# Output projection of a hybrid decoder layer by Strassen's form over quarters

## The chip, the cores and the metric

The kernel runs on one core of a Trainium2 chip. The metric is the device time of one execution in microseconds. A core has five engines with queues of their own, each of which takes its instructions strictly in order: TensorE (PE, matmuls, with PEld for the weight loads), VectorE (DVE), ScalarE (ACT), GpSimd (POOL) and SyncE (SP, which here only issues transfers). They wait for each other by semaphores. SBUF holds the operands; matmul results come in PSUM, in eight banks of 128 x 512 floats.

## The reference

One layer over 1024 tokens of width 1024, in float32. What matters here is the last product of the mixer: the outputs of eight softmax heads (NSA, 512 features) and of four gated linear-attention heads (GLA, 512 features) are joined and multiplied by one 1024 x 1024 matrix.

```python
x = x + 0.5 * swiglu_ffn(rmsnorm(x, g1), w_gate1, w_up1, w_down1)
x = x + hybrid_mixer(rmsnorm(x, gm), w_in, ..., w_out)
#     hybrid_mixer ends with
#     return jnp.concatenate([o_nsa, o_gla], axis=-1) @ w_out
x = x + 0.5 * swiglu_ffn(rmsnorm(x, g2), w_gate2, w_up2, w_down2)
return rmsnorm(x, final_norm)
```

## The kernel before

Every tensor of activations lies with features on partitions and tokens along the free axis, in two halves of 512 tokens. Each float32 operand is held as two tiles, a high part (`hi`, written by ACT as a rounded copy) and a low part (`lo`, the remainder, written by DVE as source minus high). `mm3` (L209) makes of each product three matmuls of 128 x 128 by 128 x 512: high by high, high by low, low by high.

The program runs five stages in order: FFN1 (by Strassen's form over quarters already, its weights as sums in several stages), the input projection, attention with GLA beside it, the output projection, FFN2 (Strassen's form again) with the final norm. There is no automatic scheduler: the order on every engine is the order in which the Python code issues instructions. Side work is written as generators, kept in `self.side`; `tick` steps them between blocks of matmuls, so that a `yield` puts the next step one tick later in all queues. `later(n)` puts the next n weight tiles into the queue, `fetch` starts a weight tile's load into one of three raw buffers and has ACT write the highs (L238), `settle` has DVE write the lows (L247). A weight tile is used from a ring; a slot of it is free when PE has read it for the last time.

The output projection is the loop L2246 to L2281. For each token half, and each of eight tiles of 128 output features, `fm` makes 8 x 3 matmuls into one PSUM bank, 384 in all (24 of them run early, in the attention's last part, for the GLA features, and are kept in `part`). DVE then adds the bank to the residual x (L2254), POOL adds the early part to two tiles (L2256), ACT squares the result and DVE adds the squares up (`squares`, L266 and L270) for the norm of FFN2. The tokens of half 1 are joined on the way (`joined`: high and low summed, L1482, and split anew, L1485 and L1488).

When half 0 is finished, its norm (`norm`, `rms`, `normed`) runs as side work under the matmuls of half 1. PE sums the squares over partitions (L286), DVE scales the sum (L291), POOL takes the power (L293), PE spreads it over partitions (L298), and DVE multiplies x by gain and factor (L322), then ACT and DVE split the result (L330, L331). `second` runs this for half 0 and then for half 1. FFN2's weights begin with the products for the A12 quarter, whose input is half 0 alone, so that the norm of half 1 runs under them. In FFN2, ACT L453 and DVE L456 split the weights.

## Time and profile before

| what | value |
|---|---|
| median of 3 runs | 1911.36 us (1911.22 to 1911.61) |
| the profiled execution's own time | 1911.64 us |
| its span | 1909.8 us |
| ACT busy | 46% |
| POOL busy | 11% |
| mean DMA traffic | 170 GB/s |
| attention's matmuls end | 1181.6 us |
| projection's first matmul after them to FFN2's first matmul | 1181.6 to 1264.1 us |

The span is the time from the first instruction's start to the last one's end, on the slowest core; the execution lasts 1.8 us longer than it. In a row of the profile, out<-in names the written and read tiles, "128*128" is the matmul's weight form, xN is the number of instructions, and what stands in brackets is the idle time ahead of it and what ended it. In the projection the transfers are the weights (512 KB a tile), the residual x, the joined head outputs and the stores of x.

### The profile page before, as it was taken

The page shows a single profiled execution, that of the slowest core. Times are in us where ns is not written, and L with a number is a line of the kernel's source. Part 1 is how long each engine was busy: PE and PEld are TensorE (multiplying, and loading weights), DVE is VectorE, ACT ScalarE, POOL GpSimd, SP SyncE. Part 2 cuts the span into 40 slices and gives each one's busy share as a digit, 9 for nine tenths or more (in the row PEclk, how much of TensorE's full clock was granted, in tenths as well). Part 3 has the DMA queues.
Part 4 walks back from the last instruction along what each step waited for, and adds up shares of the span by engine and source line. Part 5 has one row for each costly group of instructions (what it writes and reads, how often), then busy time and mean ns, then how long its engine had stood idle before and what let it go on. Part 6 is the DMA issues. An engine that isn't in the chain of part 4 may idle for free. (4 is left out here: it accounts for less than half of the span.)

```text
span 1909.8 us, 26312 instructions
## 1 busy us (share of the span) xinstructions
PE 1895.9 (99%) x9291; PEld 1562.8 (82%) x9291; DVE 1375.4 (72%) x2302; ACT 883.7 (46%) x1697; POOL 202.6 (11%) x259
## 2 busy tenths in 40 slices
PE   9999999999999999999999999999999999999998
PEld 7888888888888888778887888888888888888887
DVE  7977778886876762554878887557777777767766
ACT  6633333344544551323478877335333333344443
POOL 0000000000000010121445553000000000000001
PEclk9999999999999999999999999999999999999999
DMA  7434456668865230119473324544333455688652
GB/s 261 150 129 140 149 193 215 215 229 305 314 232 176 89 103 27 56 45 254 135 231 95 103 71 132 205 160 160 130 126 125 146 197 198 221 294 300 230 177 89
DMA packets 173860, 325.00 MB, mean 170 GB/s; under 512 B 17920, under 2 KB 49792, under 8 KB 173216
## 3 DMA queue, kind: packets, MB, share of 16 engines
q1 hardware_dynamic: 165152, 308.35, 47.2%
q0 software_dynamic: 2720, 10.23, 1.7%
q10 hardware_dynamic: 5856, 4.75, 0.8%
q8 instruction: 73, 1.20, 0.3%
q14 instruction: 59, 0.48, 0.1%
HBM read 234.62 MB, written 92.86 MB: 171 GB/s over the span
## 5 line engine op out<-in xcount | busy, mean ns | idle before, releaser
L211 PE MATMUL bank<-T,wt 128*128 128x512 f32 x704 | 273.9, 389 | 0.0
L212 PE MATMUL bank<-T,wt 128*128 128x512 f32 x704 | 273.9, 389 | 0.0
L213 PE MATMUL bank<-T,wt 128*128 128x512 f32 x704 | 273.9, 389 | 0.0
L211 PE MATMUL bank<-bd,wd 128*128 128x512 f32 (+1 forms) x632 | 243.0, 385 | 0.0
L213 PE MATMUL bank<-bd,wd 128*128 128x512 f32 (+1 forms) x632 | 242.5, 384 | 0.0
L212 PE MATMUL bank<-bd,wd 128*128 128x512 f32 (+1 forms) x632 | 242.5, 384 | 0.0
L211 PE MATMUL bank<-h,wt 128*128 128x512 f32 x536 | 210.1, 392 | 1.0 <-ACT wt L453 1.0
L213 PE MATMUL bank<-h,wt 128*128 128x512 f32 x536 | 209.0, 390 | 0.2
L212 PE MATMUL bank<-h,wt 128*128 128x512 f32 x536 | 208.6, 389 | 0.0
L634 ACT ACTIVATE g<-bank 128x512 f32<-128x512 f32 x88 | 52.6, 598 | 266.1 <-PE bank L213 266.0
L211 PEld LDWEIGHTS bank<-T,wt 128*128 128x128 f32 x704 | 132.2, 188 | 27.6
L213 PEld LDWEIGHTS bank<-T,wt 128*128 128x128 f32 x704 | 132.1, 188 | 27.4
L212 PEld LDWEIGHTS bank<-T,wt 128*128 128x128 f32 x704 | 132.2, 188 | 27.2
L213 PEld LDWEIGHTS bank<-bd,wd 128*128 128x128 f32 x632 | 118.8, 188 | 23.6
L212 PEld LDWEIGHTS bank<-bd,wd 128*128 128x128 f32 x632 | 118.8, 188 | 23.5
L211 PEld LDWEIGHTS bank<-bd,wd 128*128 128x128 f32 x632 | 118.8, 188 | 22.9
L453 ACT ACTIVATE wt<-v 128x512 fp32r<-128x512 f32 x176 | 109.7, 623 | 46.4 <-DVE v L418 30.1
L211 PE MATMUL bank<-h,w 128*128 128x512 f32 x312 | 124.2, 398 | 0.0
L456 DVE TENSOR_TENSOR wt<-v,wt 128x512 fp32r<-128x512 f32 x176 | 120.5, 685 | 3.5 <-ACT wt L453 3.5
L213 PE MATMUL bank<-h,w 128*128 128x512 f32 x312 | 121.8, 390 | 0.0
L212 PE MATMUL bank<-h,w 128*128 128x512 f32 x312 | 121.5, 389 | 0.0
L211 PEld LDWEIGHTS bank<-h,wt 128*128 128x128 f32 x536 | 100.7, 188 | 22.9 <-ACT wt L453 2.4
(284 smaller groups left out, 3759.7 us busy)
## 6 DMA issues: line engine op xcount, KB each, us to landing
in<-in_w_f_dram SPq DMA_DIRECT2D x132, 256.0 KB, 5.3
in<-b SPq DMA_DIRECT2D x132, 256.0 KB, 5.4
raw<-in_w_f_dram SPq DMA_DIRECT2D x44, 512.0 KB, 4.7
up<-in_w_f_dram SPq DMA_DIRECT2D x44, 512.0 KB, 5.4
raw<-in_w_in_dram SPq DMA_DIRECT2D x23, 512.0 KB, 3.8
raw<-in_w_f_dram SPq DMA_DIRECT2D x44, 256.0 KB, 4.1
b<-g SPq DMA_DIRECT2D x44, 256.0 KB, 2.1
l<-tb SPq DMA_DIRECT2D x22, 512.0 KB, 5.7
```

The source lines that it names most:

```text
L211: mm(ps, w[0], x[0], start=first, stop=False, skip_group_check=True)
L212: mm(ps, w[0], x[1], start=False, stop=False, skip_group_check=True)
L213: mm(ps, w[1], x[0], start=False, stop=last, skip_group_check=True)
L453: nc.scalar.activation(t[:, 0], a, AF.Copy)
L456: nc.vector.tensor_tensor(t[:, 1], a, t[:, 0].bitcast(F32), OP.subtract)
L634: nc.scalar.activation(dst, src, AF.Copy)
```

## The change

The projection becomes Strassen's form (in Winograd's arrangement) over the four quarters of tokens and features. With two halves of tokens and two of features (NSA and GLA), the inputs are the quarters "11" (NSA of half 0), "22" (GLA of half 1), "12" (NSA of half 1), and the sums T1 (GLA of half 0 less GLA of half 1), T3 (NSA of half 0 less GLA of half 0), T2 (T3 plus GLA of half 1) and T4 ("12" less T2). Seven products of 4 tiles x 4 contraction blocks x 3 matmuls, 48 each, take the place of eight. The code runs them in the order 1, 3, 6, 5, 7, 2, 4; product 1 has only two tiles in this stage, since the other two run early as before. A "block" here is one output tile of one product, 12 matmuls; there are 26 (1 and 2 of "22", 3 to 6 of "11", 7 to 10 of T2, 11 to 14 of T1, 15 to 18 of T3, 19 to 22 of "12", 23 to 26 of T4). Each product enters one or two quarters of x, so there are 36 additions from PSUM instead of 16, and 8 additions of `part` on POOL instead of 2.

The weight sums are taken by POOL in FFN1's second stage (`sum_up`), written to DRAM, and loaded from there: 13 weight tiles instead of 10, in a ring of four. The token sums T1, T3 and T2 are taken by POOL in the attention (`differences`) and written to DRAM; the projection's `prepare` loads them and splits them into high and low. T4, and the split of "12", are made there too. The low parts of T1 and T3 and the sums for "12" and T4 are POOL's, the lows of T2, T4 and "12" DVE's. Half 0 of x is final only when product 7 has been added, so that its norm runs under products 2 and 4. It now writes the tiles 4 to 7 first, with a pause of five ticks (`lag`) ahead of the spread, and the squares' total stands six matmuls into block 20.

In the new code the old projection loop (L2246 to L2281, in the listing above) is replaced by the one at the end of this excerpt.

```diff
-    def rms(self, st, bank=3, gap=1):
+    def rms(self, st, bank=3, gap=1, lag=2):
...
-        yield
-        yield
+        for _ in range(lag):
+            yield
...
-    def normed(self, rb, x, h, which, half, inplace=False, pace=1):
+        yield from self.rms(st, bank, gap, lag)
+        yield from self.normed(st["rb"], x, h, which, half, inplace, pace, order)
+    def normed(self, rb, x, h, which, half, inplace=False, pace=1, order=range(KT)):
...
+    def block(self, p, i, j, B, ks, first, last):
+        w = self.weight(i)[j]
+        for k in ks:
+            o = slice(k * 128, k * 128 + 128)
+            self.mm3(p, (w[:, 0, o], w[:, 1, o]), (B[k][:, 0], B[k][:, 1]), first and k == 0, last and k == 3)
+            self.tick()
...
+            spans = [f[:, k * n * 128:(k + 1) * n * 128] for k in range(len(parts))]
+            for c, pT in zip(spans, parts):
+                nc.scalar.activation(c.rearrange("p (r t) -> p r t", r=n), pT, AF.Copy)
             half, ts = i // 4, slice(i % 4 * 128, i % 4 * 128 + 128)
+            nc.sync.dma_start(gl[:, half, :, ts], f.rearrange("p (h t) -> p h t", h=4))
+            if half:
+                ot = work.tile([128, 2, 512], R32, name="ot", bufs=1)
+                self.split(ot[:, 0], ot[:, 1], f)
+                for s in range(2):
+                    nc.sync.dma_start(og_dram[1][:, s, 4:8, ts],
+                                      ot[:, s].bitcast(F32).rearrange("p (h t) -> p h t", h=4))
...
+    def differences(self, h, og, gl, td, there):
+        nc, pool = self.nc, self.nc.gpsimd
+        def both(k):
+            r = self.raw.tile([128, 1024], F32, name="raw", tag="raw").rearrange("p (i n) -> p i n", i=2)
+            nc.sync.dma_start(r, gl[:, :, k])
+            return r
+        for k in range(4):
+            r = both(k)
+            for _ in range(2):
+                yield
+            pool.tensor_tensor(r[:, 0], r[:, 0], r[:, 1], OP.subtract)
+            yield
+            nc.sync.dma_start(td[0, :, k], r[:, 0])
+        while not there():
+            yield
+        for k in range(4):
+            nc.sync.dma_start(h[k].bitcast(F32), og[:, :, k])
+        rs = {}
+        for k in range(2):
+            rs[k] = both(k)
+            yield
             yield
         for k in range(4):
             t = self.nt.tile([128, 512], F32, name="hf")
             hi, lo = [h[k][:, s] for s in range(2)]
+            pool.tensor_tensor(t, hi.bitcast(F32), lo.bitcast(F32), OP.add)
+            yield
+            yield
             nc.scalar.activation(hi, t, AF.Copy)
+            r = rs.pop(k)
+            pool.tensor_tensor(r[:, 0], t, r[:, 0], OP.subtract)
+            yield
+            yield
+            pool.tensor_tensor(r[:, 1], r[:, 0], r[:, 1], OP.add)
+            yield
+            for i in range(2):
+                nc.sync.dma_start(td[1 + i, :, k], r[:, i])
+            yield
+            pool.tensor_tensor(lo, t, hi.bitcast(F32), OP.subtract)
+            if k < 2:
+                rs[k + 2] = both(k + 2)
+            yield
+            yield
...
+                    self.away = {i: i % 4 for i in range(len(self.wproj))}
...
+            bank = self.one_bank(2)
+            self.block(bank, 0, 0, h[1], range(2), True, False)
...
+        load(1, 2)
+        part2 = self.take("A", "part", F32)
+        nc.sync.dma_start(part2, part)
+        load(0, 0)
+        load(0, 2)
+        whole = many(2, "t2f", F32)
+        for i in range(2):
+            nc.sync.dma_start(whole[i], td[2, :, 2 * i:2 * i + 2])
+        t["T2"], t["T1"] = many(4, "t2"), many(4, "t1")
...
+        def place(q, i):
+            for k in range(4):
+                nc.sync.dma_start(t[q][k][:, 1].bitcast(F32), td[i, :, k])
+        def prepare():
+            for k in range(4):
+                yield from self.eased(t["T2"][k], whole[k // 2][:, k % 2], nc.vector)
+            B["T2"] = t["T2"]
+            place("T1", 0)
+            load(1, 4)
+            load(1, 6)
+            load(0, 4)
+            load(0, 6)
+            for _ in range(4):
+                yield
+            for k in range(4):
+                yield from self.eased(t["T1"][k], None, nc.gpsimd)
+            B["T1"], t["T3"] = t["T1"], many(4, "t3")
+            place("T3", 1)
+            for k in range(4):
+                nc.sync.dma_start(t["12"][k].bitcast(F32), og[1][:, :, k])
+            load(1, 0)
+            for _ in range(8):
+                yield
+            for k in range(4):
+                yield from self.eased(t["T3"][k], None, nc.gpsimd)
+            B["T3"] = t["T3"]
+            while self.room("TA") < 4:
+                yield
+            t["T4"] = many(4, "t4")
+            for k in range(4):
+                b, t4, f = t["12"][k], t["T4"][k], self.nt.tile([128, 512], F32, name="hf")
+                hi, lo = [b[:, s] for s in range(2)]
+                nc.gpsimd.tensor_tensor(f, hi.bitcast(F32), lo.bitcast(F32), OP.add)
+                yield
+                yield
+                nc.scalar.activation(hi, f, AF.Copy)
+                nc.gpsimd.tensor_tensor(whole[k // 2][:, k % 2], f, whole[k // 2][:, k % 2], OP.subtract)
+                yield
+                nc.vector.tensor_tensor(lo, f, hi.bitcast(F32), OP.subtract)
+                yield
+                yield from self.eased(t4, whole[k // 2][:, k % 2], nc.vector)
+            self.free(*whole)
+            B.update({q: t[q] for q in ("12", "T4")})
+        return x, B, prepare(), part2, bank
+    def eased(self, t, src, eng):
+        hi, lo = [t[:, s] for s in range(2)]
+        src = lo.bitcast(F32) if src is None else src
+        self.nc.scalar.activation(hi, src, AF.Copy)
+        yield
+        eng.tensor_tensor(lo, src, hi.bitcast(F32), OP.subtract)
+        yield
...
-        self.wproj = [ins["w_out"][i % KT] for i in range(KT + 2)]
+        sums = [self.dram.tile([4, 128, 2, 512], F32, name=f"sums{i}") for i in range(2)]
+        w = ins["w_out"]
+        of = lambda t, k: [t[m:m + 2, :, k * 512:k * 512 + 512].rearrange("m p c -> p m c") for m in (0, 2)]
+        of2 = lambda i, k: [sums[i][m:m + 2, :, k].rearrange("m p c -> p m c") for m in (0, 2)]
+        self.wproj = of(w, 1)[1:] + of2(1, 0) + of2(1, 1) + of2(0, 0) + of2(0, 1) + of(w, 0) + of(w[4:], 0)
+        def sum_up(m):
+            a, b, c = [self.raw.tile([128, 1024], F32, name="raw", tag="raw").rearrange("p (i n) -> p i n", i=2)
+                       for _ in range(3)]
+            pool = nc.gpsimd
+            for t, j in ((b, m + 4), (a, m)):
+                pool.dma_start(t.rearrange("p i n -> p (i n)"), w[j])
+            pool.tensor_tensor(c[:, 0], b[:, 0], b[:, 1], OP.add)
+            pool.tensor_tensor(c[:, 1], a[:, 1], b[:, 1], OP.subtract)
+            pool.dma_start(sums[0][m], c)
+            pool.tensor_tensor(a[:, 1], c[:, 0], a[:, 1], OP.subtract)
+            pool.tensor_tensor(a[:, 0], a[:, 0], a[:, 1], OP.subtract)
+            pool.dma_start(sums[1][m], a)
...
+        for m in range(4):
+            hooks1["2", 2, 2 * m] = lambda m=m: sum_up(m)
...
+                for n, _ in enumerate(self.norm(ns3[half], x, hg, 2, half, 6 + half, True, 2, 1 + 1.4 * half,
+                                                1 - half, 2 if half else 5, range(KT) if half else EARLY)):
...
-        for half in range(2):
...
+        first3 = self.take("TA", "acc", F32)
+        ns3[0]["acc"] = first3[:, 0]
+        self.side.append(prepare)
+        halves = [slice(half * 512, half * 512 + 512) for half in range(2)]
+        def add(half, k, p, eng=nc.vector):
+            eng.tensor_tensor(x[:, k, halves[half]], x[:, k, halves[half]], p, OP.add)
+        def done(half, k):
+            self.squares(ns3[half], x, halves[half], k, nc.vector)
+            if k % 2:
+                ks = slice(k - 1, k + 1)
+                nc.sync.dma_start(xs[:, ks, halves[half]], x[:, ks, halves[half]])
+        plan = [(1, 2), (1, 3)] + [(q, m) for q in (3, 6, 5, 7, 2, 4) for m in range(4)]
+        with_, X, turn = {1: "22", 3: "11", 6: "T2", 5: "T1", 7: "T3", 2: "12", 4: "T4"}, {2: bank}, 0
+        moved = {6: (0, 0), 7: (0, 1), 8: (1, 4), 9: (1, 5), 10: (0, 4), 11: (0, 5), 14: (1, 0), 15: (1, 1)}
+        for n, (q, m) in enumerate(plan):
+            for _ in range(999):
+                if with_[q] in M:
+                    break
+                self.tick()
+            if q in (1, 6, 5):
+                if m not in X:
+                    X[m] = self.one_bank((1, 3, 2, 0)[m])
+                p = X[m]
+            elif q in (3, 7):
+                p = self.one_bank(4 + turn % 3)
+                turn += 1
+            else:
+                p = self.one_bank((1, 3, 2, 0)[m])
+            fresh = q not in (6, 5) or q == 6 and m < 2
+            self.block(p, n // 2, n % 2, M[with_[q]], range(2, 4) if n == 0 else range(4), fresh, True)
+            for half, k in {1: [(1, m)], 3: [(0, m)], 6: [(1, 4 + m)], 5: [(0, m), (0, 4 + m)],
+                            7: [(0, 4 + m), (1, 4 + m)], 2: [(1, m)], 4: [(1, 4 + m)]}[q]:
+                add(half, k, p)
+                if (q, half, k // 4) in ((5, 0, 0), (7, 0, 1), (2, 1, 0), (4, 1, 1)):
+                    done(half, k)
+            if n in moved:
+                half, k = moved[n]
+                add(half, k, part[:, k % 4], nc.gpsimd)
+            if n % 2:
+                self.later(1)
+            if m == 3 and q != 4:
+                self.free(*M.pop(with_[q]))
+            if n == 15:
+                self.free(part)
+            if q == 7 and m == 3:
                 self.drain()
+                hg[0] = [self.take("TA", "h") for _ in range(KT)]
                 self.side.append(second(x))
+            if n in (20, 21, 22):
+                ahead(n - 20)
+            if n in (23, 24):
+                step()
+                settle()
+        self.free(*M.pop("T4"))
+        hg[1] = [None] * 4 + [self.take("AT", "h") for _ in range(4)]
         self.unring()
         self.hold = (4, "A12")
         go()
```

Three places of the compiled order show how instructions moved. The first is POOL, from the end of the attention (L1528 scales the probabilities p) into the projection. Before, two additions of the early part and the power of the norm stand there:

```order
L1528 TENSOR_SCALAR p<-p,rd,gates 128x640 x4
L1528 TENSOR_SCALAR p<-p,rd,gates 128x1024 x4
L1583 DMA og_5587<-sq 64x4x128 x2
L2256 TENSOR_TENSOR x<-x,part 128x512 x2
L293 TENSOR_TENSOR r<-v,mhalf 128x4 x3
```

With the change, in the projection from the first low of T3 on (L2040, tiles t_11723 to t_11726; L2368 adds `part`, L2020 sums high and low of "12" into hf, L2024 makes T4 of it):

```order
L2040 TENSOR_TENSOR t_11723<-t_11723 128x512
L2368 TENSOR_TENSOR x<-x,part 128x512
L2040 TENSOR_TENSOR t_11724<-t_11724 128x512
L2040 TENSOR_TENSOR t_11725<-t_11725 128x512
L2368 TENSOR_TENSOR x<-x,part 128x512
L2040 TENSOR_TENSOR t_11726<-t_11726 128x512
L2020 TENSOR_TENSOR hf<-h 128x512
L2368 TENSOR_TENSOR x<-x,part 128x512
L2024 TENSOR_TENSOR t2f<-hf,t2f 128x512
L2368 TENSOR_TENSOR x<-x,part 128x512
L2020 TENSOR_TENSOR hf<-h 128x512
L2024 TENSOR_TENSOR t2f<-hf,t2f 128x512
```

Four lows of T1 and two additions of `part` stand ahead of these rows, and another six such rows for T4 and `part` behind them. The first L2024 is the ninth instruction counted from the first L2040 shown.

The second place is DVE. Before, around the end of token half 0, its list alternates between additions from a bank (L2254), sums of squares (L270) and the joining of half 1:

```order
L247 TENSOR_TENSOR w<-raw,w 128x512 x2
L1488 TENSOR_TENSOR h<-hf,h 128x512
L1482 TENSOR_TENSOR hf<-h 128x512
L1488 TENSOR_TENSOR h<-hf,h 128x512
L1482 TENSOR_TENSOR hf<-h 128x512
L2254 TENSOR_TENSOR x<-x,bank 128x512
L270 TENSOR_TENSOR acc<-acc,sq 128x512
```

With the change, near blocks 15 to 18 (L248 makes weight lows, L2026 the lows of "12", L2040 the lows of T4, L2368 adds a bank to x, L271 adds squares); two weight lows and the first T4 low (t_11823) stand just ahead:

```order
L2368 TENSOR_TENSOR x<-x,bank 128x512
L271 TENSOR_TENSOR acc<-acc,sq 128x512
L2368 TENSOR_TENSOR x<-x,bank 128x512
L2026 TENSOR_TENSOR h<-hf,h 128x512
L2040 TENSOR_TENSOR t_11824<-t2f,t_11824 128x512
L2368 TENSOR_TENSOR x<-x,bank 128x512
L271 TENSOR_TENSOR acc<-acc,sq 128x512
L2368 TENSOR_TENSOR x<-x,bank 128x512
L248 TENSOR_TENSOR w<-raw,w 128x512 x2
L2368 TENSOR_TENSOR x<-x,bank 128x512
L271 TENSOR_TENSOR acc<-acc,sq 128x512
L2368 TENSOR_TENSOR x<-x,bank 128x512
```

From the two weight lows to the last row shown there are 16 instructions; six read a bank in PSUM, ten have both inputs in SBUF. The last row is the addition that frees the bank of block 18.

The third place is PE at the sum of squares of half 0. Before, 174 matmuls of the projection stand behind it:

```order
L212 MATMUL bank<-h,w 128x512
L213 MATMUL bank<-h,w 128x512
L286 MATMUL bank<-ones,acc 128x1 x4
L211 MATMUL bank<-h,w 128x512
L212 MATMUL bank<-h,w 128x512
```

With the change it stands six matmuls into block 20:

```order
L212 MATMUL bank<-h,w 128x512
L213 MATMUL bank<-h,w 128x512
L287 MATMUL bank<-ones,acc 128x1 x4
L211 MATMUL bank<-h,w 128x512
L212 MATMUL bank<-h,w 128x512
```

Behind it there are 21 matmuls to the spread of the factor (L299), and from there 57 to FFN2's first matmul. Before, there are 24 to the spread (L298) and 150 from there.

More of the change, by code (lines that the diff above doesn't have):

```diff
@@ L58, in __init__ @@
         self.nbank = self.reserve = 0
-        self.hold, self.late, self.begun = None, False, None
+        self.hold, self.late = None, False
         self.side, self.owed, self.turn = [], 0, False
@@ L300, in rms, with norm @@
         yield
-    def norm(self, st, x, h, which, half, bank=3, inplace=False, wait=0, pace=1, gap=1):
+    def norm(self, st, x, h, which, half, bank=3, inplace=False, wait=0, pace=1, gap=1, lag=2, order=range(KT)):
         yield
@@ L308, in norm @@
             yield
-        yield from self.rms(st, bank, gap)
-        yield from self.normed(st["rb"], x, h, which, half, inplace, pace)
-    def normed(self, rb, x, h, which, half, inplace=False, pace=1):
+        yield from self.rms(st, bank, gap, lag)
+        yield from self.normed(st["rb"], x, h, which, half, inplace, pace, order)
+    def normed(self, rb, x, h, which, half, inplace=False, pace=1, order=range(KT)):
         nc = self.nc
@@ L316, in normed @@
         lows = []
-        for k in range(KT + 2):
-            if k > 1:
+        for n in range(KT + 2):
+            if n > 1:
                 lows.pop(0)()
-            if k < KT:
+            if n < KT:
+                k = order[n]
                 hf = x[:, k, ts] if inplace else self.nt.tile([128, 512], F32, name="hf")
@@ L1471, in products @@
         return lo, n, nch, s[:, :nr * nch, :w]
-    def joined(self, h, eng, every, wait):
-        nc = self.nc
-        for _ in range(wait):
+    def differences(self, h, og, gl, td, there):
[19 more added lines that the diff above has]
+            yield
             yield
@@ L1598, in first_half @@
             def first_half():
[L1599 to L1605 removed]
+                if joins and next(joins[0], joins) is joins:
+                    joins.pop()
             def scores(n):
@@ L1920, in mixer @@
                 slot[1] = "T"
-            h = [[self.take("T", "h") for _ in range(4)] + more[0]]
-            step_ends, ends = self.attention(queries, Q, pcd, K1, K2, V, og, h[0], masks, first, early, keep)
+            B = {"11": [self.take("T", "h") for _ in range(4)], "22": more[0]}
+            step_ends, ends, bank = self.attention(queries, Q, pcd, K1, K2, V, og, (B["11"], B["22"]), masks, first,
+                                                   early, keep, gl, td)
         c0.close()
@@ L1925, in mixer, with load @@
         self.open_slots(28, "A")
-        h.append([self.take("A", "h") for _ in range(KT)])
+        many = lambda n, name, dt=R32: [self.take("TA", name, dt) for _ in range(n)]
+        t = {"12": many(4, "h")}
         x = new_x()
-        load = lambda half, k: nc.sync.dma_start(x[:, k:k + 2, half * 512:half * 512 + 512],
-                                                 xs[:, k:k + 2, half * 512:half * 512 + 512])
+        def load(half, k, n=2):
+            ts = slice(half * 512, half * 512 + 512)
+            nc.sync.dma_start(x[:, k:k + n, ts], xs[:, k:k + n, ts])
         self.raws(1)
-        for k in range(0, KT, 2):
-            load(0, k)
-            if k == 0:
-                pt = self.take("A", "part", F32)
-                nc.sync.dma_start(pt, part)
+        load(1, 2)
[7 more added lines that the diff above has]
+        t["T2"], t["T1"] = many(4, "t2"), many(4, "t1")
         while ends:
```

107 lines of the change are left out of this document (24 added, 83 removed).

## The prediction

> **What bounds the kernel now.** I read the page first: busy time by engine, the forty slices, then the waits of PE and the windows around the projection.
>
> ```profile
> span 1909.8 us, 26312 instructions
> PE 1895.9 (99%) x9291; PEld 1562.8 (82%) x9291; DVE 1375.4 (72%) x2302; ACT 883.7 (46%) x1697; POOL 202.6 (11%) x259
> PE   9999999999999999999999999999999999999998
> PEclk9999999999999999999999999999999999999999
> ```
>
> PE is busy for 99% of the span at an undiminished clock, in every slice. The windows show the same beside the change (from:to, length, then busy time of PE, PEld, DVE, ACT, POOL, then PE's clock, DMA share, GB/s); PE's waits say how little it stands still.
>
> ```profile
> 1181.00:1222.00 41.00, 41.00 (x181) 33.46 (x180) 24.17 (x37) 15.37 (x27) 4.24 (x4) 1.00 0.88 323
> 1222.00:1265.00 43.00, 43.00 (x199) 35.85 (x198) 23.21 (x38) 12.62 (x21) 1.05 (x1) 1.00 0.30 98
> ...
> PE pair L1461 <- ACT p L1518: 1.6, 4, 0.7
> PE bank L211 <- ACT wt L453: 1.0, 3, 0.4
> ```
>
> So the projection (1181 to 1264) is bound by matmuls, with DVE at 59% and 54%. A matmul less is time saved, and every microsecond in which PE waits for DVE or ACT is time added. The question is whether PE stays fed.
>
> **What is removed.** PE's list loses 48 matmuls (16 × 24 become 7 × 48; the compiled order is shorter by as many, so that the change does not do this is no rival). What one costs is read from starts:
>
> ```profile
> 1261.62 0.39 PE L212 MATMUL bank<-h,w 128*128 128x512 f32 x1
> ...
> 1267.97 0.39 PE L213 MATMUL bank<-h,wt 128*128 128x512 f32 x1
> ```
>
> Between these two starts lie 28 matmuls: 6.35 / 28 = 0.2268 us each (0.39 is latency). 48 × 0.2268 = **10.9 us saved**. A block of 12 matmuls takes 2.72 us.
>
> **What is added on DVE and POOL, by one clock.** Zero is the start of the first block after the last attention product. Of blocks 1 and 2, six matmuls were done early, so 18 are left (4.1 us); block j ≥ 3 starts at 4.1 + 2.72(j − 3) unless stalled: block 9 at 20.4, block 18 at 44.9. Rows for the side work:
>
> ```profile
> 1236.11 0.74 DVE L322 SCALAR_TENSOR_TENSOR x<-x,gains,bank 128x512 f32<-128x512 f32 x1
> 1236.77 0.68 DVE L331 TENSOR_TENSOR h<-x,h 128x512 fp32r<-128x512 f32 x1
> 1237.37 0.74 DVE L322 SCALAR_TENSOR_TENSOR x<-x,gains,bank 128x512 f32<-128x512 f32 x1
> ...
> 1182.27 3.23 ACT L238 ACTIVATE w<-raw 128x512 fp32r<-128x512 f32 x6
> ...
> L2254 DVE TENSOR_TENSOR x<-x,bank 128x512 f32<-128x512 f32 x16 | 10.9, 683 | 15.2 <-PE bank L213 15.2
> ```
>
> From start to start, a scaled product takes 0.66 us on DVE, an add or subtract 0.60, and an ACT copy 3.23 / 6 = 0.54. The x-add from PSUM has the same 0.68 us duration, so 0.60 too. A POOL add of this size, alone and in a row, and beside DVE:
>
> ```profile
> 1084.41 1.28 POOL L1488 TENSOR_TENSOR h<-hf,h 128x512 fp32r<-128x512 f32 x1
> 1085.64 1.30 POOL L1482 TENSOR_TENSOR hf<-h 128x512 f32<-128x512 f32 x1
> ...
> 1086.06 1.29 DVE L1558 TENSOR_TENSOR pt<-bank,pt 128x512 fp32r<-128x512 f32 x2 [0.19 <-ACT pt L1556]
> ...
> 1185.93 2.38 DVE L247 TENSOR_TENSOR w<-raw,w 128x512 fp32r<-128x512 f32 x2
> 1193.67 1.29 DVE L247 TENSOR_TENSOR w<-raw,w 128x512 fp32r<-128x512 f32 x2 [0.66 <-ACT w L238]
> ...
> 1186.16 1.61 POOL L2256 TENSOR_TENSOR x<-x,part 128x512 f32<-128x512 f32 x1 [2.15 <-issue]
> 1188.99 1.29 POOL L2256 TENSOR_TENSOR x<-x,part 128x512 f32<-128x512 f32 x1 [1.23 <-DVE x L2254]
> ```
>
> POOL takes 1.29 us. Two DVE weight lows, whose inputs both lie in SBUF, take 1.29 us alone and 2.38 beside a POOL add, which itself takes 1.61. The pair at 1086.06, with an input in PSUM, keeps 1.29 beside POOL. So POOL and a two-SBUF DVE instruction seem to exclude each other: in the stalled pair 1186.16 + 1.61 = 1187.77 is POOL's end, 1188.31 DVE's, 0.55 us later, one DVE instruction. The projection had two such POOL adds; now POOL has 24 in it (8 part adds, 8 lows of T1 and T3, 4 sums of "12", 4 of T4).
>
> The Trainium skill, "SBUF — State Buffer", section "Who interferes with whom", says that a VectorE instruction with two SBUF inputs contends with a GpSimd one that reads SBUF, each blocking the other entirely; it speaks against this change. The rows 2.38 against 1.29 agree. By it the sum is the forecast below, without it rival B.
>
> *Stall 1, block 18.* The third product's three x banks rotate, so block 18 takes block 15's bank after DVE's x-add. That add stands behind this chain. ACT's highs of T3 queue behind two weight copies that wait for block 8's end (20.4), since the ring has four tiles: 2 × 0.54 and a first high of 0.6 later, at 22.1, POOL's first T3 low can start. To the first T4 sum POOL has 9 instructions: 9 × 1.29 = 11.6, plus 4 two-SBUF DVE instructions let in between, 4 × 0.55 = 2.2: 35.9. ACT then does T4's high, a square and two weight copies (1.8 with the last one's end): 37.7. From the weight lows on, DVE has 16 instructions to that add, ten with two SBUF inputs. Unhindered: 16 × 0.60 = 9.6. Excluded: 10 × 0.55 + 8 further POOL instructions × 1.29 = 15.8, the six PSUM adds lying beneath; the add ends at 53.5, so PE waits 53.5 − 44.9 = **8.6**. With no exclusion anywhere it ends at 22.1 + 11.6 + 1.8 + 9.6 = 45.1: 0.2. I take 8.6, since the row for exactly this pair of engines is 2.38; both ends stay for the range. Queued behind the waiting add on DVE are the remaining adds, the lows of "12" and T4 and the sum of squares, and PE waits for those next.
>
> *Stall 2, inside block 20.* All of half 0 now becomes final in block 18, and its sum of squares (L287) stands six matmuls into block 20. From that add on DVE has 18 instructions to the total, 18 × 0.60 + 0.4 of waits for squares = 11.2; PE has 2.72 + 2.72 + 1.36 = 6.8 to do: **4.4**. Bounds: 0 if DVE comes in with the later adds done, 7 if two more POOL sums (2 × 1.29) hold it.
>
> *Stall 3, FFN2's first product.* Its weight copy on ACT stands behind the squares and highs of half 0's norm.
>
> ```profile
> 1229.19 1.05 PE L298 MATMUL bank<-ident,r 128*128 128x128 f32 x8
> 1229.99 0.48 PE L211 MATMUL bank<-h,w 128*128 128x512 f32 x1
> ...
> 1230.33 0.75 DVE L322 SCALAR_TENSOR_TENSOR x<-x,gains,bank 128x512 f32<-128x512 f32 x1 [1.85 <-issue]
> ```
>
> DVE begins the norm 0.34 us after PE resumes. Then 8 × 0.66 + 13 × 0.60 = 13.1, 0.3 of waits, 1.2 for ACT's square and copy: 14.9, against 57 matmuls = 12.9 left on PE: **2.0** (0 to 4). Before, half 1's 192 matmuls covered this norm; now only blocks 19 to 26 do.
>
> *Stall 4.* Half 1's norm starts as late; its sum of squares waits in FFN2's second product: **0.9** more than the 1.0 us of waits for L453 above (0 to 2).
>
> **What costs nothing, and its cover.** The weight sums add 16 POOL instructions and 8 MB of transfers in FFN1's second stage, under PE:
>
> ```profile
> 330.00:420.00 90.00, 90.00 (x399) 74.53 (x398) 73.88 (x116) 35.37 (x63) 2.02 (x6) 1.00 0.58 199
> 1080.00:1130.00 50.00, 50.00 (x322) 41.43 (x321) 42.66 (x79) 40.61 (x85) 30.28 (x30) 1.00 0.20 50
> ```
>
> DVE is at 82% there and POOL nearly idle; 16 × 1.29 = 20.6 us of POOL can hold DVE for about that, spread over loads issued several steps ahead; 90 us hold 16 us of free DVE. If the cover fails, 2 us. POOL's twelve extra sums in the attention fall where POOL is at 61% and DVE's matrix work reads PSUM; without that cover POOL's scalings of p come late, up to 3 us. Weights go from 10 tiles to 13:
>
> ```profile
> raw<-in_w_out_dram SPq DMA_DIRECT2D x7, 512.0 KB, 5.6
> h<-og SPq DMA_DIRECT2D x8, 512.0 KB, 8.4
> ```
>
> A tile lands in 5.6 us and serves two blocks, 5.4 us, with three loads in flight on SP's queue: covered. The early x loads that made the DMA share 0.88 are spread later. If transfers fall to 8.4 us each, the T1 and T3 loads (one after another on SP) put stall 1 back by up to 3 us.
>
> **Sum.** 8.6 + 4.4 + 2.0 + 0.9 = 15.9 us of stalls against 10.9 saved: +5.0. The profiled execution took 1911.64 us (span 1909.8, 1.8 around it), 0.3 above the median of 1911.36: 1916.6 profiled, **1916.4** against the median.
>
> **Rivals.** *B, the exclusion is worth little:* the POOL work mostly falls where DVE waits anyway, as in the attention rows. Stall 1 is 0.2, stalls 2 to 4 remain: −10.9 + 7.5 = −3.4, 1908.0. Against it: DVE's list there has hardly a gap. *C, the other side: DVE keeps ahead.* If DVE reaches block 15's add by 44.9 with the later x-adds already done, and the total of squares comes within block 20, PE never stops and the count alone decides: −10.9, 1900.5. It turns on 11.2 us of DVE work fitting into 6.8, so DVE would have to enter block 18 some 4.4 us ahead. For it: DVE was only 54 to 59% busy. Against it: the adds go from 16 to 36 and meet the lows of T4 and "12" in one place. *D, the stall slows PE's clock.*
>
> ```profile
> 1.01 3.77 PE L100 MATMUL bank<-blank 128*128 128x512 bf16 x9 [1.01 <-DVE mhalf L106]
> 1902.46 0.71 PE L298 MATMUL bank<-ident,r 128*128 128x128 f32 x4 [0.21 <-POOL r L293]
> ...
> 1905.00:1909.80 4.80, 0.00 (x0) 0.00 (x0) 0.67 (x2) 0.00 (x0) 0.76 (x2) 0.57 0.66 219
> ```
>
> Soon after PE's last matmul the granted clock is 0.57, and a cold start runs at 3.77 / 9 = 0.42 us per matmul. After a gap of 8.6 us some 10 to 20 matmuls could cost 0.19 more each, and with slower transfers 3 more: +2 to +6, 1918 to 1922. The Trainium skill, "TensorE: Matmul & The Clock Gate", Part 1, has an idle window of about 3.4 us drop the clock to half; the row 0.57 agrees.
>
> **How the numbers follow.** A measurement of this kernel tells 0.2%, 3.8 us, from no change: 1907.5 to 1915.2 is the same. Chances: the forecast 0.52 (of it 0.14 below 1915.2, when stall 1 is 2 us or more shorter), B 0.23 (0.06 below 1907.5), C 0.13, D 0.12. Slower 0.38 + 0.12 = 0.50, same 0.14 + 0.17 = 0.31, faster 0.06 + 0.13 = 0.19. The range leaves out most of C and the last of D: 1905 to 1921; the forecast's own range is 1912 to 1920.
>
> **What would show it.** PE busy falls by about 10.9 us, and PE's waits name DVE's x-add as releaser of a wait near 8.6 us in front of block 18, DVE's squares for L287 (4.4) and the weight copy for FFN2's first matmul (2). DVE's two-SBUF rows there last more than 1 us each, POOL's 1.6 or more. A PE without waits in blocks 17 to 20 makes C; waits of 4 and 2 but none at block 18 make B; a clock under 1.00 after the gap makes D. New waits in FFN1 or the attention would break the covers.

## The result and the profile after

The changed kernel takes 1924.85 us (median of 4 runs, 1923.14 to 1925.51) against 1911.48 us before: ratio 1.0067, with a 95% interval of 1.005 to 1.0085. It is slower by 13.4 us where 5.0 were forecast. The profiled execution took 1924.24 us, its span is 1922.5 us. First its page:

```profile
span 1922.5 us, 26555 instructions
PE 1891.8 (98%) x9243; PEld 1556.8 (81%) x9243; DVE 1414.3 (74%) x2319; ACT 898.8 (47%) x1723; POOL 283.3 (15%) x325
...
PE   9999999999999999999999999899999999999998
...
PEclk9999999999999999999999999899999999999999
```

The nines have one gap, in slice 26, in PE's row and in the clock's (PEclk, the share of full speed that was granted to PE). PE's waits in this kernel, and the stretch of the projection (windows, before and then after):

```profile
PE bank L211 <- DVE x L2368: 10.5, 2, 9.1
PE bank L211 <- ACT wt L455: 2.3, 3, 1.9
PE bank L287 <- DVE acc L276: 2.2, 2, 1.5
...
PE bank L1587 <- POOL p L1566: 1.2, 2, 0.8
...
1182.00:1262.00 80.00, 80.00 (x360) 65.99 (x359) 46.70 (x72) 27.76 (x48) 5.29 (x5) 1.00 0.58 207
...
1182.00:1262.00 80.00, 67.92 (x286) 55.06 (x285) 60.16 (x79) 32.81 (x58) 38.40 (x27) 0.91 0.62 220
```

In the same 80 us PE does 286 matmul rows instead of 360, DVE is busy for 60 us instead of 47 and POOL for 38 instead of 5. (DVE's additions from PSUM are 34 in the trace, and not 36 as counted ahead; no term of the sum rests on it.) FFN1's second stage, where the weight sums are taken, has not changed: PE is busy for 90.00 of 90 and 200.00 of 200 us, as before.

The place of the longest wait, in the timeline (start, duration): POOL's first low of T3 and its first T4 sum, DVE's rows to the addition that frees the bank, PE's block 18, and DVE's total of squares.

```profile
1209.40 1.30 POOL L2040 TENSOR_TENSOR t<-t 128x512 fp32r<-128x512 f32 x1 [1.67 <-ACT t L2038]
1220.29 1.76 POOL L2024 TENSOR_TENSOR t2f<-hf,t2f 128x512 f32<-128x512 f32 x1
...
1223.79 3.17 DVE L248 TENSOR_TENSOR w<-raw,w 128x512 fp32r<-128x512 f32 x2 [1.70 <-ACT w L239]
1234.84 2.82 DVE L248 TENSOR_TENSOR w<-raw,w 128x512 fp32r<-128x512 f32 x2
1238.78 0.67 DVE L2368 TENSOR_TENSOR x<-x,bank 128x512 f32<-128x512 f32 x1
1250.09 0.69 DVE L276 TENSOR_TENSOR acc<-acc,sq 128x512 f32<-128x512 f32 x1
...
1239.51 0.80 PE L211 MATMUL bank<-t,w 128*128 128x512 f32 x1 [9.08 <-DVE x L2368]
...
1239.50:1245.20 5.70, 5.69 (x13) 4.47 (x14) 5.62 (x10) 2.28 (x6) 0.00 (x0) 0.50 0.27 95
```

From the weight lows at 1223.79 to the end of the freeing addition at 1239.45 DVE needs 15.7 us for its 16 instructions (15.8 in the forecast): pairs of weight lows last 2.8 to 3.2 us instead of 1.29. PE waits 9.1 us, and then runs block 18 at a granted clock of 0.50, its matmuls 0.43 us apart instead of 0.23. "Half clock" stands for such a spell below.

Where DVE's list begins can be read from the chain of work that ended last: the loads of T1 and then of T3 lie on it (start, time to landing). ACT's copies just ahead of T3's lows wait for a weight tile, and then for T3:

```profile
1189.17 8.36 DMA t<-td
...
1203.77 6.84 DMA t<-td
...
1206.43 1.15 ACT L239 ACTIVATE w<-raw 128x512 fp32r<-128x512 f32 x2 [4.59 <-DMA raw<-sums]
1208.69 1.91 ACT L2038 ACTIVATE t<-t 128x512 fp32r<-128x512 f32 x3 [1.11 <-DMA t<-td]
```

Where the 12.7 us between the two spans come from, by the starts of PE's matmuls in both traces (a matmul at full clock counted as 0.2268 us):

| term | forecast | measured |
|---|---|---|
| 48 matmuls less | −10.9 | −10.9 |
| attention ends later (1183.6 against 1181.6) | 0 | +2.1 |
| wait in front of block 6 | 0 | +1.7 |
| wait in front of block 18 | +8.6 | +9.2 |
| half clock in block 18 | 0 | +2.8 |
| wait for half 0's sum of squares | +4.4 | +1.7 |
| half clock after it | 0 | +1.7 |
| FFN2's first product | +2.0 | +2.4 |
| half 1's sum of squares, small waits | +0.9 | +0.6 |
| from PE's last matmul to the end | 0 | +1.4 |
| sum | +5.0 | +12.7 |

The rows follow PE. The waits at blocks 6 and 18, the half clock in block 18 and the wait for half 0's squares all lie ahead of the same total of DVE's: together 15.4 us, for 13.0 in the forecast.

### The profile page after: what moved, and what is told of

Read it like the earlier page. It is cut to its first block, busy times and chain, and to the rows that moved or that the text cites. A ratio compares the mean times of both kernels' runs of the same rounds, so it can differ in the third digit from the quotient of the medians.

```text
span 1922.5 us, 26555 instructions
## 1 busy us (share of the span) xinstructions
PE 1891.8 (98%) x9243; PEld 1556.8 (81%) x9243; DVE 1414.3 (74%) x2319; ACT 898.8 (47%) x1723; POOL 283.3 (15%) x325
## 4 chain that ended last, share of the span: by engine, by line
PE 89%; DVE 4%; DMA 2%; issue 1%; POOL 1%; ACT 1%; SPq 0%; ACTq 0%; POOLq 0%; DVEq 0%
PE bank L211 24%; PE bank L213 24%; PE bank L212 24%; PE pair L1468 3%; PE bank L1587 3%; PE bank L990 2%; PE bank L992 2%; PE bank L991 2%; PE bank L1605 1%; PE bank L1606 1%; DMA t<-td 1%; DVE w L248 1%; DMA raw<-gl 1%; PE pair L1476 0%; PE bank L1187 0%
## 5 line engine op out<-in xcount | busy, mean ns | idle before, releaser
L455 ACT ACTIVATE wt<-v 128x512 fp32r<-128x512 f32 x176 | 109.9, 624 | 84.9 <-PE bank L213 66.9
L294 POOL TENSOR_TENSOR r<-v,mhalf 128x4 f32<-128x4 f32 (+1 forms) x9 | 9.7, 1078 | 856.6 <-DVE v L292 856.6
L211 PEld LDWEIGHTS bank<-h,wt 128*128 128x128 f32 x536 | 100.8, 188 | 24.6 <-ACT wt L455 4.3
L213 PEld LDWEIGHTS bank<-h,wt 128*128 128x128 f32 x536 | 100.7, 188 | 22.5 <-DVE wt L458 1.6
L406 DVE TENSOR_TENSOR bd<-in,bd 128x512 fp32r<-128x512 f32 x154 | 110.7, 720 | 10.8 <-ACT bd L748 10.8
```

The lines of the kernel that those rows point to most:

```text
L211: mm(ps, w[0], x[0], start=first, stop=False, skip_group_check=True)
L213: mm(ps, w[1], x[0], start=False, stop=last, skip_group_check=True)
L406: minus = lambda o, p, q: nc.vector.tensor_tensor(o, p, q, OP.subtract)
L455: nc.scalar.activation(t[:, 0], a, AF.Copy)
```

## The experiments

Times are medians; the kernel before took 1911.4 to 1911.8 us beside each group. Each expectation numbers its own theories. In the text "theory 1" without more is the one behind them all: DVE's list, lengthened by POOL's use of SBUF, is the bound from the projection's middle to half 0's norm.

**One more bank.** The rotation of x banks gets bank 7:

```diff
-                p = self.one_bank(4 + turn % 3)
+                p = self.one_bank(4 + turn % 4)
```

> The third product and the first in this loop rotate over four banks of x instead of three, so that block 18 no longer waits for block 15's addition, nor block 6 for block 3's. Theory 1 (DVE's list is the bound from block 15 on; the bank is only where PE meets it): DVE's work is unchanged, so the total of squares comes as late as before; the wait of 9.1 us in front of block 18 becomes one of 9 to 13 us in front of the sum of squares in block 20. The time falls by block 6's 1.5 us, and by 0 to 2 more: 1921 to 1924. Theory 2 (the bank is the bound): the 9.1 us go and most of the half-clock matmuls with them: 1909 to 1914.

Measured 1925.42 (1924.93 to 1926.24), ratio to before 1.0074 [1.0059, 1.0089]: no gain. PE's waits:

```profile
PE bank L211 <- ACT h L2023: 4.8, 2, 2.6
PE bank L212 <- DVE h L2026: 4.1, 1, 4.1
PE bank L287 <- DVE acc L276: 3.6, 2, 2.9
```

The waits in front of blocks 6 and 18 are gone whole, and 11.8 us of waits stand in their place in blocks 19 and 20: 8.9 for the highs and lows of "12" and 2.9 for the total of squares. (The other 0.7 on L287 is half 1's.) Counted from the projection's first matmul, the total was done 0.3 us earlier, at 66.9 instead of 67.1. The bank was only where PE met DVE; theory 2 falls. Theory 1 was too good by a microsecond or more: behind the total the clock stood at one half for 6.83 us, instead of 3.41 in the changed kernel.

**All of POOL's work on DVE.** `nc.gpsimd` becomes `nc.vector` in the lows of T1 and T3, the sums of "12" and T4, and the additions of `part`.

> All 24 additions and subtractions that POOL does in the projection (lows of T1 and T3, sums of '12' and T4, the early part) are done by DVE. Theory 1 (a DVE instruction with two SBUF inputs and a POOL one exclude each other): DVE gets 24 x 0.60 = 14.4 us more of work, but loses about 12 us by which its rows with two SBUF inputs are longer than 1.29 a pair or 0.68 alone in the changed kernel; and the chain to the first T4 sum is shorter, since its nine operations take 0.60 instead of 1.29 to 1.7. The rows are 0.68 again; the time falls by 1 to 6 us: 1919 to 1924. Theory 2 (the exclusion costs little, the list of DVE is only too long): 5 to 14 us more, 1930 to 1939.

Measured 1922.48 (1921.79 to 1924.01), 1.0060 [1.0043, 1.0077]. DVE gets 24 instructions more and the time falls by 2.4 us (the two groups of four runs overlap from 1923.1 to 1924.0). The group of the weight lows in the changed kernel, and then here (busy, mean ns, idle before):

```profile
L248 DVE TENSOR_TENSOR w<-raw,w 128x512 fp32r<-128x512 f32 x24 | 24.2, 1056 | 5.9 <-ACT w L239 5.7
...
L248 DVE TENSOR_TENSOR w<-raw,w 128x512 fp32r<-128x512 f32 x24 | 15.3, 686 | 3.7 <-ACT w L239 3.6
```

The same 24 instructions take 24.2 us beside POOL and 15.3 without it, though nothing in them changed. The x-adds, with an input in PSUM, kept 677 against 679 ns.

**Matmuls of zeros in the gap.**

```diff
+            if n == 17:
+                self.warm(self.one_bank(7), 36)
```

> 36 matmuls on a tile of zeros, into a bank that nothing reads, stand in front of block 18 (36 x 0.227 = 8.2 us of the 9.1 us in which PE waits there). Theory 1 (PE's clock falls because PE stood still): block 18 runs at 0.227 us per matmul instead of 0.425, which saves 2.8 us, and if the second spell of half clock belongs to the first, 1.6 more; part of it comes back as a longer wait for the sum of squares, since DVE's list is the bound: 1921 to 1924. Theory 2 (the clock falls for another reason): block 18 stays at 0.42, time unchanged at 1925.

Measured 1927.27 (1926.15 to 1927.94), 1.0082 [1.0067, 1.0097]: 2.4 us slower than the changed kernel, a miss for both of its theories.

```profile
1239.88 0.50 PE L211 MATMUL bank<-t,w 128*128 128x512 f32 x1 [1.68 <-DVE x L2368]
1251.20 1.87 PE L287 MATMUL bank<-ones,acc 128*128 128x1 f32 x8 [4.21 <-DVE acc L276]
```

Block 18 ran at full clock, as its theory 1 says, but PE only came to the sum of squares earlier and stood there for 4.2 us (1.5 in the changed kernel); the sum itself started 0.4 us later than there (1250.83). After it came 6.83 us at half clock, for 3.41 in the changed kernel. So half clock in block 18 cost nothing, as PE had to wait for DVE anyway; half clock behind the sum of squares, with the norm waiting for PE's next steps, counts. It isn't all of the difference: of the 2.5 us between the two profiled spans 1.2 lie between the projection's first matmul and FFN2's; 0.6 lie ahead of it and 0.6 in FFN2, where the edit changes nothing.

**The attention's loads one tile ahead.**

```diff
-            r = both(k)
+            r, nxt = nxt, both(k + 1) if k < 3 else None
```

> In the attention, each load for a difference of the GLA halves is issued one tile ahead, so that POOL doesn't stand before the subtraction until its load lands. Theory 1 (POOL's 2.87 us of waiting for the load holds the scalings of p queued behind it, and PE for these): the attention ends 1.5 to 2.1 us earlier, 1922.8 to 1923.4. Theory 2 (POOL's twelve additional operations themselves hold the scalings): within 0.5 us of 1924.9.

Measured 1923.06 (1922.71 to 1923.53), 1.0061 [1.0046, 1.0076]: 1.8 us faster. POOL's fourth subtraction in the changed kernel, and here:

```profile
1018.65 1.30 POOL L1494 TENSOR_TENSOR raw<-raw 128x512 f32<-128x512 f32 x1 [2.87 <-DMA raw<-gl]
...
1014.51 1.29 POOL L1495 TENSOR_TENSOR raw<-raw 128x512 f32<-128x512 f32 x1
```

It was the wait for a load, with the scalings of p queued behind it, and not POOL's additional work: the attention ends at 1181.6 again, as before.

**Fewer additions of the early part, and combinations.** In e5 ACT copies `part` into the accumulating banks. As run, e5, e6 and e8 leave the early part out of six of its eight places: the next matmul, without a start flag, overwrote what ACT had written. The Trainium skill, "PSUM — Partial Sum Buffer", section "Terms", says that only TensorE changes the bit by which a matmul adds or overwrites; the lost values agree. The times are those of the instructions named.

> The early part of tiles 0 and 1 is copied by ACT into the two banks in which products 6 and 5 accumulate, so that six of POOL's eight additions of the early part fall away (two, to x of half 1, stay). DVE's list is unchanged; ACT gets two copies more. Between the first low of T3 and the first T4 sum POOL then has 6 operations instead of 9. Theory 1 (POOL's operations delay the T4 chain and lengthen DVE's rows): the first T4 sum comes 4 us or more earlier, DVE's pair rows near block 15 are shorter, and the waits in front of block 18 and of the sum of squares fall by 3 to 6 us together: 1919 to 1922. Theory 2 (the number of DVE's instructions alone sets the total of squares): 1924 to 1925.5.

1920.43 (1919.21 to 1921.85), 1.0047 [1.0032, 1.0062]: 4.4 us faster with DVE's list unchanged, the wait in front of block 18 5.2 us. Theory 1. With the part brought in whole, by PE:

```diff
+                        nc.tensor.matmul(X[m], self.ident, part[:, m], start=True, stop=False, skip_group_check=True)
```

> The changed kernel with one edit: the early part comes into the two banks by PE's two float32 matmuls with the identity, so that six of POOL's eight additions of it fall away and the result is whole. Theory 1: as e5_preset, whose time was 1920.4, with 2 us more of PE's work ahead of block 18, where PE waits anyway: 1919.5 to 1921.5. Theory 2 (PE's work is the bound): 1922 to 1927.

1921.17 (1919.95 to 1924.79), 1.0053 [1.0039, 1.0067]: as theory 1.

> Three edits together: the preset banks of e5_preset, the remaining POOL operations of the projection on DVE (e2_on_dve), and the attention's loads one tile ahead (e4_ahead). Theory 1: e2 gave 2.4 us and e4 1.8; without the six additions DVE has 18 instructions more than in the changed kernel instead of 24, 3.6 us less than in e2, of which 2 to 3.6 count: 1917 to 1919. If the six additions were not on the path, only the two known gains show: 1920 to 1921.

1917.98 (1917.73 to 1918.93), 1.0034 [1.0021, 1.0047]: 6.9 us better than the changed kernel. Alone, e2 gave 2.4, e4 1.8 and e5 4.4; e2 and e5 shorten the same list, so their gains don't add. From the projection's first matmul to FFN2's, the trace has 85.9 us here and 85.7 in e5: with the six additions gone, it made no difference to this stretch whether the other 18 operations were POOL's or DVE's.

> Half 0's spread of the norm factor (L299) stands 15 matmuls behind its sum of squares instead of 21. Theory 1 (from the total of squares on, the path is sum of squares, spread, norm on DVE, weight copy on ACT, FFN2's first product; PE's own matmuls lie beside it): the spread comes 1.4 to 2.5 us earlier (6 matmuls at 0.227 to 0.425), the wait for the weight copy at FFN2's first matmul grows by what PE has less to do in between, and the time falls by 1.4 to 2.5: 1922.3 to 1923.5. Theory 2 (PE's matmuls from there to FFN2 are the bound): unchanged, 1924.9.

1925.36 (1923.93 to 1927.19), 1.0073 [1.0058, 1.0088]: no gain, a miss. The spread came 0.9 us earlier, but FFN2's first matmul began at 1274.08 instead of 1274.10. In the changed kernel DVE does an x-add and a sum of squares of half 1 before the spread; here it does them after, so its list up to the weight copy ends at the same time. The spread starts that list in both; what it gained went to the two instructions put behind it.

> All together: e6_all, the lag of three (e7_lag3) and four x banks in rotation (e1_four_banks). Theory 1: DVE's list from block 9 to the norm of half 0 is the bound; e6's time less 1.4 to 2.5 for the lag, less up to 1 for the banks (block 6's wait): 1914.5 to 1917. It stays slower than the kernel before, since DVE's list with 36 additions from PSUM and the lows of '12' and T4 still ends later than PE.

1917.64 (1916.13 to 1918.64), 1.0032 [1.0021, 1.0044]: a miss, as nothing beyond e6 can be told.

**Squares summed by PE.** Seven additions leave DVE's list; PE multiplies each tile of squares of half 0 by ones, two blocks later:

```diff
-            self.squares(ns3[half], x, halves[half], k, nc.vector)
+            if half:
+                self.squares(ns3[half], x, halves[half], k, nc.vector)
+            else:
+                sq = self.nt.tile([128, 512], F32, name="sq")
+                nc.scalar.activation(sq, x[:, k, halves[0]], AF.Square)
+                pend.append((n, sq))
...
+            flush(n - 2)
```

Two things more differ from e6: PE brings in the early part, as in e11, and the spread stands 12 matmuls behind the sum of squares instead of 21.

> PE puts the early part of tiles 0 and 1 into the two banks by two matmuls with the identity in float32 (about 2 us of PE, in place of ACT's copies of e5_preset, whose values the next product overwrote), the other POOL operations of the projection are on DVE (e2_on_dve), the attention's loads come one tile ahead (e4_ahead), the spread of half 0's factor comes 12 matmuls behind its sum of squares, and PE sums half 0's squares itself, one tile at a time two blocks later, so that DVE loses seven additions. Theory 1 (DVE's list is the bound up to the sum of squares): e6_all's 1918.0, less 7 x 0.60 = 4.2 us for DVE's additions, less 1 to 2 for the earlier spread: 1911.5 to 1914. If PE's own matmuls (2 us for the part, 3 for the squares) are on the path instead: 1917 to 1920.

1913.45 (1913.08 to 1914.22; 5 rounds), 1.0009 [1.0, 1.0018]: 4.5 us better than e6, the largest step. A shorter way to the spread alone had brought nothing (e7), nor PE's part anything over ACT's (e11 against e5), so that the squares are the likely cause; no run has them alone. PE's waits for DVE in the projection shrink to one of 1.1 us, no half clock is left, and PE's own work shows instead: 0.9 us for each of the eight sums.

> e9_squares, but with the lows of T1 and T3, the sums of '12' and T4 and two additions of the early part left on POOL. Theory 1 (a POOL operation costs DVE its whole 1.29 us where DVE has two SBUF inputs, and nothing where DVE reads PSUM): DVE has 18 instructions (10.8 us) less than in e9, and its rows beside POOL are longer by about as much: between 1 us faster and 4 us slower than e9, 1911 to 1917. If the exclusion were not there: 5 us or more faster than e9.

1913.42 (1912.54 to 1914.83), 1.0009 [1.0001, 1.0018]: the same time. It can't tell what POOL's 18 operations cost DVE, nor refute the case without exclusion, since PE is the bound: behind block 6 it waits for DVE in neither version up to FFN2. DVE's busy time tells more (sums of 1181.6 to 1263, e9 and then here):

```profile
sum 81.40, PE 80.10 PEld 65.98 DVE 65.92 ACT 38.79 POOL 2.38; mean PE 20.02 PEld 16.49 DVE 16.48 ACT 9.70 POOL 0.59
...
sum 81.40, PE 80.31 PEld 66.34 DVE 62.41 ACT 38.35 POOL 29.37; mean PE 20.08 PEld 16.59 DVE 15.60 ACT 9.59 POOL 7.34
```

DVE has 18 instructions less, 10.8 us at 0.60 each, and is busy for 3.5 us less.

> From e9_squares: the early part of tiles 0 and 1 is added once by DVE to the bank in which products 6 and 5 accumulate (2 DVE additions in place of PE's two identity matmuls); PE sums five tiles of squares instead of eight (DVE adds up the first four, in blocks 11 to 14, where it has gaps); the first product in the loop rotates over four banks, so that block 6 doesn't wait; the lows of T1 and T3 are POOL's again, in a stretch where DVE has gaps, and the sums of '12' and T4 stay DVE's. Theory 1 (PE and DVE now take nearly the same time, so that what PE no longer has to do counts as long as DVE keeps up): PE has 1.7 us less for the part, 3 x 0.9 less for squares, 1.1 less of waiting for block 6: 5.5 us, 1908 from e9's 1913.45; if DVE is late by up to 4 us, 1908 to 1912. If DVE is the bound as in the changed kernel, waits in front of block 18 to 20 come back and the time is 1913 or more.

1916.40 (1916.01 to 1917.84), 1.0027 [1.0016, 1.0037]: a miss for its theory 1. The time is that of its last case, but the wait stands elsewhere than in front of blocks 18 to 20, at PE's sum of the first four squares:

```profile
PE bank L2382 <- DVE acc L2395: 5.0, 1, 5.0
```

Behind it the clock stands at one half for 6.83 us. DVE adds up squares right behind ACT, 0.7 us of idle time each, and two pairs of weight lows beside POOL take 3.1 and 3.0 us again.

> From e9_squares: the early part of tiles 0 and 1 is added once by DVE to the bank of products 6 and 5 instead of PE's two identity matmuls (1.7 us of PE, for 1.2 of DVE at a place where DVE has gaps), and the first product in the loop rotates over four banks (block 6's wait of 1.1 us). Theory 1 (in e9 PE and DVE take nearly the same time, PE a little more): 1 to 2.8 us faster than e9's 1913.45: 1910.6 to 1912.5, the kernel before's own time. If DVE is the bound there already: 1913 to 1914.

1910.92 (1910.47 to 1911.38), 0.9996 [0.9987, 1.0005]: the best version, and the same as the kernel before. From the first block to FFN2's first matmul PE stands still nowhere for DVE:

```profile
PE bank L211 <- ACT wt L459: 1.7, 4, 0.8
PE pair L1472 <- ACT p L1561: 1.6, 4, 0.7
...
1181.80:1260.60 78.80, 78.01 (x380) 65.32 (x378) 67.08 (x110) 39.26 (x68) 2.38 (x3) 1.00 0.68 240
```

That stretch took 82.5 us before, 90.5 with the change, and takes 78.8 here: 3.7 of the 10.9 us saved are left. The rest is PE's sums of squares (eight of 0.9 us for the one that stood there before) and 0.8 us of waiting for a weight copy. The whole isn't 3.7 us faster, since FFN2 takes 637.0 us from its first matmul to its last instead of 635.0, and the end 1.3 us more (below). Of FFN2's 2.0 us, 0.8 is a wait for half 1's total of squares; the rest stays open.

> From e14_nine: the first four tiles of squares of half 0 are added in two pairs by DVE, one block after the second square of each pair is there, so that PE sums six tiles instead of eight. PE has 2 x 0.9 us less to do ahead of the sum of squares, DVE two additions (1.2 us) more. If PE is the bound in e14: 1.8 us faster, 1909.1. If DVE is as near to its bound as its 35.3 us of work in the 40 us from 1200 to 1240 suggest: waits on DVE come back, and the time stays within 1 us of 1910.9, or goes up.

1911.83 (1911.11 to 1912.87), 1.0002 [0.9993, 1.0011]: 0.9 us slower than e14.

```profile
PE bank L2387 <- ACT sq L2398: 2.0, 1, 2.0
```

1.2 us of additions on DVE bring back a wait of 2.0 us for a square, which waits for DVE's x-add. DVE and PE bind each other here.

**The end of the program.** In the kernel before, each small store of constants by POOL in FFN1 stands twice:

```diff
         self.nc.gpsimd.dma_start(getattr(self, n)[b], src[b])
+        self.nc.gpsimd.dma_start(getattr(self, n)[b], src[b])
```

> The kernel before with one edit: in FFN1 POOL issues each of its sixteen small stores of constants twice, so that it issues sixteen transfers more, as many as the changed kernel's weight sums add; no other instruction changes. Theory 1 (POOL's drain at the end of the program takes longer the more transfers POOL has issued): the drain, 5.41 us in the kernel before and 6.71 in the changed one, takes about 6.7, the time from PE's last matmul to the end 8.7 us instead of 7.3, and the whole 1.0 to 1.4 us more: 1912.6 to 1913.1. Theory 2 (the longer end has another reason): within 0.4 us of the kernel before.

1913.13 (1912.56 to 1913.34, and one run of 4905.19), 1.0007 [0.9998, 1.0016]: 1.65 us above the kernel before, whose median beside it was 1911.48, a little more than expected. The time from PE's last matmuls to the end, in the kernel before, the changed one and here:

```profile
1902.46:1909.80 7.34, 0.71 (x4) 0.52 (x4) 2.33 (x6) 0.38 (x1) 2.09 (x3) 0.72 0.58 193
...
1913.79:1922.50 8.71, 0.71 (x4) 0.52 (x4) 2.05 (x5) 0.38 (x1) 2.09 (x3) 0.72 0.49 162
...
1902.38:1911.10 8.72, 0.71 (x4) 0.52 (x4) 2.34 (x6) 0.38 (x1) 2.09 (x3) 0.75 0.49 162
```

With sixteen more transfers issued by POOL in FFN1, some 1500 us earlier, the end is as long as in the changed kernel. In the traces POOL's closing drain lasts 5.41 us before and 6.71 in the other two.

## Why the prediction was wrong, and where it was right

The direction and the main mechanism were right: DVE's list, lengthened beside POOL, holds PE. The last leg of **stall 1** came as worked out, DVE's 16 instructions in 15.7 us for 15.8. That POOL's work lengthens them is shown by e2, where the same rows are short again. That the bank isn't the cause is shown by e1. That the wait itself came out at 9.2 us for 8.6 is partly luck. On the forecast's clock, from the projection's first matmul (1183.64), the freeing addition ended at 55.8 us instead of 53.5, but PE too was late for block 18, at 46.6 instead of 44.9, since it had stood in front of block 6. The two delays nearly cancel in the wait.

**Stalls 2 to 4** had the right sum, with block 18's half clock counted in (7.5 us for 7.3), and another split. After a full-clock block 18 (e3) the wait for the sum of squares is 4.2 us, for 4.4 forecast; in the changed kernel most of it was spent as half clock in block 18. FFN2's first product was 2.4 for 2.0, by the path that was given: from PE's first matmul behind the spread (1259.04) to FFN2's first (1274.10) it took 15.1 us, for 14.9.

What failed is the step **"what costs nothing, and its cover"**, and with it the sum. It named most of these covers and what their failure would cost, but put all of them at nothing in the sum. Three of its terms were not nothing.

- *The attention's sums.* They were covered by POOL's free time, read from 1080 to 1130 us. Four of the twelve ran at 994 to 1020 us, and the queue was not read for what a subtraction that waits for its load holds up: 2.1 us, which e4 gives back (1.8 in the time).
- *The loads at the projection's start.* "A tile lands in 5.6 us", so covered; T1 and T3 were given up to 3 us in the range alone. Their loads took 8.36 and 6.84 us and lie on the chain that ended last. POOL's first low of T3 began at 25.8 us instead of 22.1, and the total of squares was done at 67.1 instead of 53.5 + 11.2 = 64.7: 2.4 us. This is read from the trace; no run moved these loads. The wait of 1.7 us in front of block 6, the fourth in a rotation of three banks, was overlooked as well, but isn't a cost of its own: without it (e1) the total came only 0.3 us earlier.
- *The sixteen transfers.* They were priced in FFN1 alone, where they do cost nothing; 1.4 us of them came at the end of the program (e13).

The second fault was to set **the clock** apart as rival D with a chance of 0.12, while the forecast itself had a gap of 8.6 us and quoted the row with 0.57. The clock did fall, and where DVE's list is the bound it cost nothing in block 18; the spell behind the sum of squares cost 1.7. The Trainium skill, "TensorE: Matmul & The Clock Gate", Part 1, has the clock fall after an idle window of about 3.4 us. By these runs less is enough: a gap of 2.1 us in e6 and the 1.5 us ahead of the changed kernel's sum of squares were each followed, a microsecond after PE had resumed, by a spell of half clock, while the 2.0 us in e15 were not. A gap's length alone doesn't decide: the 1.86 us ahead of FFN2's first matmul were followed by such a spell in e6 and not in the changed kernel.

2.1 + 2.4 + 1.4 + 1.7 us are 7.6 of the 7.7 between the two sums. FFN2's first product (0.4 too little) and half 1's sum of squares (0.3 too much) make up the rest.

Rival B (the exclusion is worth little) had 0.2 us for stall 1, and falls with the 9.2 measured and with e2's rows. In e5 and e11, six POOL additions fewer and DVE's list unchanged make 4.4 and 3.7 us; how much of it comes through shorter rows on DVE, and how much through the shorter chain to T4 on POOL, isn't separated. Rival C (the count alone) needs a DVE that keeps up; e14 nearly makes one, and then the sums of squares that had to go to PE eat most of the count.

## What to carry to other kernels

Removing matmuls pays only while the engine that evacuates keeps up: 47 us of DVE under 80 of PE looked like room, but 18 x-adds and the lows of two token sums more, with fewer matmuls above them, made DVE the bound, and work moved to POOL gave DVE little of its time back (3.5 of 10.8 us in e10). Where one engine's list is the bound, a wait that is taken away comes back at the next place where the engines meet; price the list, and not the waits. And each moved operation is to be priced with what stands behind it in its queue, loads included.

## What was not expected of the hardware

POOL's closing drain took 5.41 us, and 6.71 with sixteen transfers more, both when these were the changed kernel's weight sums and when they were e13's constants in FFN1. Around the projection the clock's records hold spells of one half of 3.41 (e6), 6.83 (e5), 10.24 (the changed kernel) and 13.65 us (e4), whole multiples of 3.41, though the gaps before them were of any length. Summing a 128 x 512 tile of squares by four matmuls with one column each takes 0.9 us of PE (in e15 from 1229.75 to the next matmul at 1230.66), as much as four full 128 x 512 matmuls. And a matmul without a start flag overwrote a bank that ACT had filled, while one behind a DVE addition in place (e14) to a bank that PE had written added to it.
